# The row of RMSNorm factors from diagonal matrices instead of a power over 256 values: one core of a Trainium2 chip

## The chip, the cores and the metric

The kernel runs on one core of one Trainium2 chip. The metric is the device time in microseconds. Before the change three runs took 1470.35 us in the median.

## The reference

One decoder layer over 256 tokens (SEQ = 256) with D_MODEL = 2048, all in float32. The part that matters here is the head of the layer:

```python
def rmsnorm(x, g):
    y = x * rsqrt(mean(x * x, axis=-1) + EPS)
    return y * g

h = rmsnorm(x, norm1_g)
proj = h @ w_in
qkv, z, b_raw, a_raw, u_raw, v_raw, ga_raw, gb_raw = split(proj)
qkv = silu(causal_dwconv(qkv, dn_conv_w))
...
u = gelu(u_raw)
vg = layernorm(gelu(v_raw), sg_ln_g, sg_ln_b)
ws = where(lower triangle, sg_w, 0)
mixed = einsum(ws, vg per chunk of 128 tokens and group of 128 channels) + sg_b
y_b = u * mixed
```

Behind it follow a gated DeltaNet over q, k and v, the projections of both branches, their gated merge, an output projection, a second RMSNorm with a gated MLP, and a last RMSNorm.

The norm's factor of a token is one number, `rsqrt(mean(x*x) + EPS)`, so it is multiplied in after the projection: for products with tokens on the partitions as a column (128 partitions, one column for each of the two tiles of 128 tokens), for products with channels on the partitions as a row of 256 values that is the same on all partitions.

## The kernel before

Tokens stand in NT = 2 tiles of 128, D_MODEL in NK = 16 blocks of 128. Each float32 operand is split in a rounded part and a residual (`w_hi`, `w_lo` of the weights; the two halves of `x_h` of the activations), and a product is made of three matmuls (L153, L154, L155). The weights come through three buffers `w_raw` of 1 MB; ScalarE makes `w_hi` (L124), VectorE `w_lo` (L127), for two blocks of D_MODEL at a time. A *step* is the work on two such blocks: for u and its neighbours twelve matmuls, three for each of two blocks and two tiles of tokens. There are four buffers of `w_hi` and four of `w_lo`.

The program starts with `vg_pass`, the product for v, which also loads x, splits it, and sums its squares in `xss` (128 partitions x 2 x 256 tokens, so the sum over partitions is still missing). Then `norm1` makes the factors, in two forms. The columns `rstd1` (128x2): four small matmuls with `xss` as the stationary operand (L306), VectorE's scale and EPS (`rs_v`, L266), and a power of -0.5 on GpSimd (L267). The row `rrow` (128x256): two matmuls with a matrix of ones as the stationary operand (L303), VectorE's `rrow_v` (L312), and a power over 256 values on each partition on GpSimd (L313).

Behind it stand the four Gelu of v (L360, which need `rstd1`), VectorE's statistics of the layernorm (L361, L365), and the factor of the layernorm, `sg_rs`, again by a small power on GpSimd (L267). The ten pieces of the layernorm on VectorE (two of L372, which need `sg_rs`, and eight of L381) are written between the steps of the next product, `bau`, which has three groups: the first with 348 columns (b, a and the start of u, "u's opening group"), then two with 346. After the opening group VectorE writes `ba` (L398) and ScalarE the Gelu of u (L401); GpSimd masks the mixing matrices `ws` (L406, after their load, L405), TensorE transposes them (L412), ScalarE copies them out (L413). After the second and third group come the mixing matmuls (L421).

`rrow` is used first in the product for q, k and v, where GpSimd multiplies it in (L201 in `chan_evict`), and `pre` is the buffer of that place, whose first columns GpSimd sets to zero (L476). The second norm, far behind, makes its row in another way: `row_broadcast` (L269) multiplies the identity by a column, which gives a diagonal matrix (`dg`, L274), multiplies that by ones on TensorE (L277), so that each partition gets the whole row, and copies it out of PSUM on ScalarE (L278).

Each engine takes its instructions in order. That order is made by the tile framework's scheduler, which may place an instruction ahead of its place in the text when its own estimate says so. A wait for a value holds everything behind it on the same engine. All loads are issued by the queue of SyncE, in order.

Of the kernel before, what the change touches and what calls it, by code (L numbers as in the profile page):

```python
# [9 lines left out]
F32 = mybir.dt.float32  # L10
F32R = mybir.dt.float32r
AF = mybir.ActivationFunctionType
ALU = mybir.AluOpType
# [3 lines left out]
P = 128  # L17
D = 2048
T = 256
NT = T // P  # L20
# [9 lines left out]
EPS = 1e-6  # L30
# [68 lines left out]
def decoder_kernel(ctx: ExitStack, tc: tile.TileContext, a: dict):  # L99
    nc = tc.nc  # L100
    out = a["out"]

    const = ctx.enter_context(tc.tile_pool(name="const", bufs=1))
# [5 lines left out]
    aux = ctx.enter_context(tc.tile_pool(name="aux", bufs=4, space=PSUM))  # L109

    def bank(pool, name):
        return pool.tile([P, 512], F32, name=name, tag="bank")
# [17 lines left out]
    def source(name, g):  # L130

        cols = GROUPS[name]
        return a["w_" + name], sum(n for _, n in cols[:g]), cols[g][1]
# [23 lines left out]
    def tok_steps(x, src, n_k, name):  # L157

        ps = [bank(acc, f"{name}{t}")[:, 0 : src[2]] for t in range(NT)]
        for k0, n, hi, lo in stream(src, n_k):  # L160
            tok_mms(ps, x, n_k, k0, n, hi, lo)
            yield
        return ps

    def finish(steps):

        while True:
            try:
                next(steps)
            except StopIteration as e:  # L170
                return e.value
# [63 lines left out]
    cm = {n: cst[:, 128 * i : 128 * (i + 1)] for i, n in enumerate(CONSTS)}  # L235
    base = 128 * len(CONSTS)
    for i, n in enumerate(CONSTS64):
        cm[n] = cst[:, base + 64 * i : base + 64 * (i + 1)]
    neg_half = const.tile([P, 2 * H], F32, name="neg_half")
    nc.gpsimd.memset(neg_half, -0.5)  # L240
    eps_t = const.tile([P, 1], F32, name="eps_t")
    nc.gpsimd.memset(eps_t, EPS)
    rstd1 = const.tile([P, NT], F32, name="rstd1")
    rrow = const.tile([P, T], F32, name="rrow")

    sg_ctx = ExitStack()
# [5 lines left out]
    x_pool = x_ctx.enter_context(tc.tile_pool(name="x_t", bufs=1))  # L252
    x_t = x_pool.tile([P, NK, T], F32, name="x_t")
    xss = x_pool.tile([P, 2, T], F32, name="xss")
# [7 lines left out]
    def rsqrt_small(dst, src, scale):  # L262

        n = src.shape[-1]
        v = small.tile([P, n], F32, name="rs_v", tag=f"rs_v{n}")
        nc.vector.tensor_scalar(v, src, scalar1=scale, scalar2=EPS, op0=ALU.mult, op1=ALU.add)  # L266
        nc.gpsimd.tensor_tensor(dst, v, neg_half[:, 0:n], op=ALU.pow)  # L267

    def row_broadcast(dst, col):  # L269

        ps = bank(aux, "ps_row")
        for t in range(NT):
            dg = small.tile([P, P], F32, name="dg", tag="dg")
            nc.vector.tensor_scalar(  # L274
                dg, cm["ident"], scalar1=col[:, t : t + 1], scalar2=None, op0=ALU.mult
            )
            nc.tensor.matmul(ps[:, t * P : (t + 1) * P], lhsT=cm["ones"], rhs=dg, start=True, stop=True)  # L277
        nc.scalar.copy(dst, ps[:, 0:T])  # L278
# [19 lines left out]

    def norm1():

        ps = bank(aux, "ps_row")
        for i in range(2):
            nc.tensor.matmul(ps[:, 0:T], lhsT=cm["ones"], rhs=xss[:, i, :], start=i == 0, stop=i == 1)  # L303
        for t in range(NT):
            for i in range(2):
                nc.tensor.matmul(  # L306
                    ps[:, T + t : T + t + 1], lhsT=xss[:, i, t * P : (t + 1) * P], rhs=cm["ones"][:, 0:1],
                    start=i == 0, stop=i == 1,
                )
        rsqrt_small(rstd1, ps[:, T : T + NT], 1.0 / D)  # L310
        v = x_pool.tile([P, T], F32, name="rrow_v")
        nc.vector.tensor_scalar(v, ps[:, 0:T], scalar1=1.0 / D, scalar2=EPS, op0=ALU.mult, op1=ALU.add)  # L312
        nc.gpsimd.tensor_tensor(rrow, v, neg_half[:, 0:1].broadcast_to([P, T]), op=ALU.pow)  # L313

    def vg_pass():

# [28 lines left out]
    nc.sync.dma_start(ln_g, a["sg_ln_g"].partition_broadcast(P))  # L345
    nc.sync.dma_start(ln_b, a["sg_ln_b"].partition_broadcast(P))
    norm1()
    x_ctx.close()

# [3 lines left out]
    with sg_ctx:  # L353
        vg = sg.tile([P, NT, SGW], F32, name="vg")
        st = sg.tile([P, NT, 2, 6], F32, name="st")
        ws_t = sg.tile([P, NG, P], F32, name="ws_t")
        for c in range(2):
            for t in range(NT):
                o = vg[:, t, 512 * c : 512 * (c + 1)]
                nc.scalar.activation(o, ps_vg[c][t], AF.Gelu, scale=rstd1[:, t : t + 1])  # L360
                nc.vector.bn_stats(st[:, t, c, :], o)  # L361

        mv = sg.tile([P, NT, 2], F32, name="mv")
        for t in range(NT):
            nc.vector.bn_aggr(mv[:, t, :], st[:, t].rearrange("p c s -> p (c s)"))  # L365
        rs = sg.tile([P, NT], F32, name="sg_rs")
        rsqrt_small(rs, mv[:, :, 1], 1.0)

        def norm():

            for t in range(NT):
                nc.vector.tensor_scalar(  # L372
                    vg[:, t, :], vg[:, t, :], scalar1=mv[:, t, 0:1], scalar2=rs[:, t : t + 1],
                    op0=ALU.subtract, op1=ALU.mult,
                )
                yield
            for t in range(NT):
                for q in range(2):
                    qs = slice(512 * q, 512 * (q + 1))
                    for tab, op in ((ln_g, ALU.mult), (ln_b, ALU.add)):  # L380
                        nc.vector.tensor_tensor(vg[:, t, qs], vg[:, t, qs], tab[:, qs], op=op)  # L381
                        yield

        pieces = norm()
        ug = sg.tile([P, NT, SGW], F32, name="ug")
        for c, (start, width) in enumerate(GROUPS["bau"]):
            steps = tok_steps(x_h, source("bau", c), NK, "ps_u_")
            for _ in range(3 if c == 0 else 0):
                next(steps)
            for _ in range((5, 5, 0)[c]):  # L390
                next(pieces)
                next(steps)
            ps = finish(steps)
            n0 = max(0, C_U - start)
            u0 = start + n0 - C_U
            for t in range(NT):
                if n0:
                    nc.vector.tensor_scalar(  # L398
                        ba[:, t], ps[t][:, 0:n0], scalar1=rstd1[:, t : t + 1], scalar2=None, op0=ALU.mult
                    )  # L400
                nc.scalar.activation(  # L401
                    ug[:, t, u0 : u0 + width - n0], ps[t][:, n0:], AF.Gelu, scale=rstd1[:, t : t + 1]
                )
            if c == 0:
                nc.sync.dma_start(ws, a["sg_w"].rearrange("g i j -> i g j"))  # L405
                nc.gpsimd.affine_select(  # L406
                    ws, ws, pattern=[[0, NG], [-1, P]], compare_op=ALU.is_ge, fill=0.0, base=0, channel_multiplier=1
                )
                for q in range(2):
                    pw = bank(aux, "ps_ws")  # L410
                    for g in range(4):
                        nc.tensor.transpose(pw[:, g * P : (g + 1) * P], ws[:, 4 * q + g, :], cm["ident"])  # L412
                    nc.scalar.copy(ws_t[:, 4 * q : 4 * q + 4, :], pw.rearrange("p (g i) -> p g i", g=4))  # L413
                continue
            for t in range(NT):
                uh = ug[:, t, 512 * (c - 1) : 512 * c]
                pm = bank(aux, "ps_mix")
                for g in range(4):
                    gg = 4 * (c - 1) + g
                    gs = slice(g * P, (g + 1) * P)  # L420
                    nc.tensor.matmul(  # L421
                        pm[:, gs], lhsT=ws_t[:, gg, :], rhs=vg[:, t, gg * P : (gg + 1) * P], start=True, stop=True
                    )
                for g in range(4):
                    gg = 4 * (c - 1) + g
                    gs = slice(g * P, (g + 1) * P)
                    nc.vector.scalar_tensor_tensor(
                        uh[:, gs], pm[:, gs], sgbt[:, gg : gg + 1], uh[:, gs], op0=ALU.add, op1=ALU.mult
                    )
                to_chan(uh, y_b, t, 4 * (c - 1))  # L430
# [423 lines left out]
    for c in range(4):  # L854
        cs = slice(512 * c, 512 * (c + 1))
        ps = finish(wo_steps if c == 0 else tok_steps(x_m, source("out", c), NK, "ps_wo"))
# [18 lines left out]
    for f in range(0, NF, 2):  # L875
        ps = chan_group(x_h2, source("gu", f // 2), "ps_gu")
# [6 lines left out]
        for i in range(2):  # L883
# [8 lines left out]
            for j in range(2):  # L892
                nc.vector.scalar_tensor_tensor(
                    cv, gu[:, 0, 2 + j : 2 + j + T], fcw[:, 3 * ff + j : 3 * ff + j + 1], cv,
                    op0=ALU.mult, op1=ALU.add,
# [130 lines left out]
```

## Time and profile before

| | |
|---|---|
| three runs | 1470.35 us median, 1468.33 to 1471.92 |
| profiled execution | 1468.47 us, span of the core 1466.7 us |
| mean granted TensorE clock | 0.985 |
| busy: TensorE, VectorE, ScalarE, GpSimd | 1420.0, 899.5, 717.6, 266.1 us |
| read from HBM | 263.73 MB, 181 GB/s over the span |

The span runs from the first to the last instruction; the time of an execution has 1.8 us more around it. A row of the timeline is: start in us, duration in us, engine, line of the kernel, operation, output <- inputs, form, count, and in brackets how long the engine was idle before and who released it. A row of the waits is: who waited <- for whom, total us, times, longest us. In the groups of one line, three numbers are the shortest, median and longest duration in ns, then the first and last start in us. PE is TensorE, PEld its weight loads, DVE VectorE, ACT ScalarE, POOL GpSimd.

### The profile page before, as it was taken

What the parts mean: (1) busy time and instruction counts of PE and PEld (TensorE: products, weight loads), DVE (VectorE), ACT (ScalarE), POOL (GpSimd) and SP (SyncE); (2) the same over time, 40 slices, a digit from 0 to 9 for tenths busy, and PEclk for the clock granted to TensorE, in tenths of its full rate; (3) what the DMA queues carried; (4) which work ended last, traced back from release to release, by engine and by line L of the source; (5) the groups of instructions that cost most, each with busy time, mean ns of one, the idle gap of its engine ahead of it and who ended that gap; (6) DMA issues with size and microseconds to landing.
All of it is one profiled execution on the core that took longest, in us unless ns stands there. A gap on an engine that the chain in (4) does not pass through costs nothing.

```text
span 1466.7 us, 19565 instructions
## 1 busy us (share of the span) xinstructions
PE 1420.0 (97%) x7784; PEld 1211.3 (83%) x7784; DVE 899.5 (61%) x1128; ACT 717.6 (49%) x979; POOL 266.1 (18%) x214
## 2 busy tenths in 40 slices
PE   9739999999999999999999999999999999999997
PEld 7639888888788888888888888888888888888886
DVE  7335687868745654565557666566666666545455
ACT  7314665654344354445555555555555455444444
POOL 0560121221102200110013123122132131000002
PEclk9859999999999999999999999999999999999999
DMA  8516455444543355575555555555555555555552
GB/s 291 179 58 204 173 192 184 173 170 147 198 144 123 111 197 193 183 261 195 179 194 175 199 191 183 202 180 193 195 180 199 184 189 200 186 191 197 199 185 105
DMA packets 46620, 267.10 MB, mean 182 GB/s; under 512 B 4800, under 2 KB 12736, under 8 KB 16960
## 3 DMA queue, kind: packets, MB, share of 16 engines
q1 hardware_dynamic: 46096, 264.79, 51.4%
q8 instruction: 61, 1.00, 0.3%
q10 hardware_dynamic: 432, 1.06, 0.2%
q14 instruction: 31, 0.25, 0.0%
HBM read 263.73 MB, written 2.10 MB: 181 GB/s over the span
## 4 chain that ended last, share of the span: by engine, by line
PE 92%; issue 3%; DVE 3%; POOL 1%; DMA 0%; ACT 0%; POOLq 0%; DVEq 0%; SPq 0%
PE ps_gu L186 22%; PE ps_gu L189 11%; PE ps_qkv L186 6%; PE ps_dn L919 5%; PE ps_dn L920 5%; PE ps_dn L918 5%; PE ps_gate L153 4%; PE ps_gate L154 3%; PE ps_gate L155 3%; PE ps_qkv L189 3%; PE ps_wo L155 2%; PE ps_wo L154 2%; PE ps_wo L153 2%; PE ps_br L154 2%; PE ps_br L153 2%
## 5 line engine op out<-in xcount | busy, mean ns | idle before, releaser
L127 DVE TENSOR_TENSOR w_lo<-w_raw,w_hi 128x1024 fp32r<-128x1024 f32 (+3 forms) x412 | 529.8, 1290 | 360.8 <-ACT w_hi L124 358.5
L124 ACT CAST w_hi<-w_raw 128x1024 fp32r<-128x1024 f32 (+3 forms) x411 | 421.5, 1027 | 493.9 <-PE ps_gu L186 156.7
L186 PE MATMUL ps_gu<-x_h,w_hi 128*128 128x512 f32 x1408 | 488.5, 394 | 0.0
L189 PE MATMUL ps_gu<-x_h,w_lo 128*128 128x256 f32 x1408 | 391.3, 278 | 0.0
L186 PEld LDWEIGHTS ps_gu<-x_h,w_hi 128*128 128x128 f32 x1408 | 264.5, 188 | 61.0
L189 PEld LDWEIGHTS ps_gu<-x_h,w_lo 128*128 128x128 f32 x1408 | 264.6, 188 | 0.0
L127 DVE TENSOR_TENSOR w_lo<-wd_raw,w_hi 128x1024 fp32r<-128x1024 f32 x84 | 104.2, 1240 | 105.2 <-ACT w_hi L124 105.2
L124 ACT CAST w_hi<-wd_raw 128x1024 fp32r<-128x1024 f32 x84 | 88.6, 1054 | 120.3 <-PE ps_dn L920 113.1
L186 PE MATMUL ps_qkv<-x_h,w_hi 128*128 128x512 f32 x384 | 133.6, 395 | 0.0
L920 PE MATMUL ps_dn<-w_hi,y_s 128*128 128x512 f32 x336 | 130.9, 390 | 0.0
L918 PE MATMUL ps_dn<-w_hi,y_s 128*128 128x512 f32 x336 | 130.9, 390 | 0.0
L919 PE MATMUL ps_dn<-w_lo,y_s 128*128 128x512 f32 x336 | 130.9, 390 | 0.0
L201 POOL TENSOR_TENSOR gu<-gu,rrow 128x512 f32<-128x512 f32 x44 | 61.4, 1396 | 337.1 <-DVE gu L200 316.1
L189 PE MATMUL ps_qkv<-x_h,w_lo 128*128 128x256 f32 x384 | 106.8, 278 | 0.0
L153 PE MATMUL ps_gate<-w_hi,x_h 128*128 128x512 f32 x256 | 102.2, 399 | 0.0
L154 PE MATMUL ps_gate<-w_lo,x_h 128*128 128x512 f32 x256 | 100.2, 391 | 0.4 <-DVE w_lo L127 0.4
L155 PE MATMUL ps_gate<-w_hi,x_h 128*128 128x512 f32 x256 | 99.9, 390 | 0.0
L186 PEld LDWEIGHTS ps_qkv<-x_h,w_hi 128*128 128x128 f32 x384 | 72.2, 188 | 16.5
L918 PEld LDWEIGHTS ps_dn<-w_hi,y_s 128*128 128x128 f32 x336 | 63.1, 188 | 13.2
L919 PEld LDWEIGHTS ps_dn<-w_lo,y_s 128*128 128x128 f32 x336 | 63.1, 188 | 13.0
L920 PEld LDWEIGHTS ps_dn<-w_hi,y_s 128*128 128x128 f32 x336 | 63.1, 188 | 13.0
L189 PEld LDWEIGHTS ps_qkv<-x_h,w_lo 128*128 128x128 f32 x384 | 72.2, 188 | 0.2
(266 smaller groups left out, 1872.4 us busy)
## 6 DMA issues: line engine op xcount, KB each, us to landing
w_raw<-in_w_gu SPq DMA_DIRECT2D x88, 1024.0 KB, 4.8
wd_raw<-in_ffn_w_down SPq DMA_DIRECT2D x44, 1024.0 KB, 4.8
w_raw<-in_w_qkv SPq DMA_DIRECT2D x24, 1024.0 KB, 4.8
w_raw<-in_w_gb SPq DMA_DIRECT2D x16, 1024.0 KB, 4.8
w_raw<-in_w_ga SPq DMA_DIRECT2D x16, 1024.0 KB, 4.8
w_raw<-in_w_out SPq DMA_DIRECT2D x16, 1024.0 KB, 4.8
w_raw<-in_w_branch_b SPq DMA_DIRECT2D x8, 1024.0 KB, 4.8
w_raw<-in_w_z SPq DMA_DIRECT2D x8, 1024.0 KB, 4.8
```

What stands on the lines that cost most here:

```text
L124: nc.scalar.copy(hi, raw)
L127: nc.vector.tensor_tensor(lo, raw, f32(hi), op=ALU.subtract)
L153: nc.tensor.matmul(ps[t], lhsT=xh, rhs=hi[:, j, :], start=(k == 0), stop=False)
L154: nc.tensor.matmul(ps[t], lhsT=xh, rhs=lo[:, j, :], start=False, stop=False)
L155: nc.tensor.matmul(ps[t], lhsT=xl, rhs=hi[:, j, :], start=False, stop=(k == n_k - 1))
L186: nc.tensor.matmul(ps[m], lhsT=hi[:, j, ms], rhs=xk, start=(k == 0), stop=(k == NK - 1), skip_group_check=True)
L189: nc.tensor.matmul(ps[m][:, 0:T], lhsT=lo[:, j, ms], rhs=xk[:, 0:T], start=False, stop=(k == NK - 1), skip_group_check=True,)
L201: nc.gpsimd.tensor_tensor(dst, dst, bc(rrow, 1, 2), op=ALU.mult)
L918: nc.tensor.matmul(o, lhsT=yh, rhs=hi[:, cs], start=(k == 0), stop=False)
L919: nc.tensor.matmul(o, lhsT=yh, rhs=lo[:, cs], start=False, stop=False)
L920: nc.tensor.matmul(o, lhsT=yl, rhs=hi[:, cs], start=False, stop=(k == NF - 1))
```

## The change

The factors' row is no longer computed for itself. `norm1` keeps only the columns, with a new one-column constant `one_c` in place of a column of the loaded ones. After u's opening group `row_broadcast`, which the second norm has used already, makes the row from the two columns of `rstd1`. Two operations on `rstd1` before anything needs it (a product, and a power on two values) run at the program's start; their result is overwritten.

```diff
+    one_c = const.tile([P, 1], F32, name="one_c")
+    nc.gpsimd.memset(one_c, 1.0)
     neg_half = const.tile([P, 2 * H], F32, name="neg_half")
...
     rstd1 = const.tile([P, NT], F32, name="rstd1")
+    nc.gpsimd.tensor_tensor(rstd1, neg_half[:, 0:1].broadcast_to([P, NT]), neg_half[:, 0:NT], op=ALU.mult)
+    nc.gpsimd.tensor_tensor(rstd1, rstd1, neg_half[:, 0:NT], op=ALU.pow)
...
     def norm1():
 
-        ps = bank(aux, "ps_row")
-        for i in range(2):
-            nc.tensor.matmul(ps[:, 0:T], lhsT=cm["ones"], rhs=xss[:, i, :], start=i == 0, stop=i == 1)
+        ps = bank(aux, "ps_ss")
         for t in range(NT):
             for i in range(2):
                 nc.tensor.matmul(
-                    ps[:, T + t : T + t + 1], lhsT=xss[:, i, t * P : (t + 1) * P], rhs=cm["ones"][:, 0:1],
+                    ps[:, t : t + 1], lhsT=xss[:, i, t * P : (t + 1) * P], rhs=one_c,
                     start=i == 0, stop=i == 1,
                 )
-        rsqrt_small(rstd1, ps[:, T : T + NT], 1.0 / D)
-        v = x_pool.tile([P, T], F32, name="rrow_v")
-        nc.vector.tensor_scalar(v, ps[:, 0:T], scalar1=1.0 / D, scalar2=EPS, op0=ALU.mult, op1=ALU.add)
-        nc.gpsimd.tensor_tensor(rrow, v, neg_half[:, 0:1].broadcast_to([P, T]), op=ALU.pow)
+        rsqrt_small(rstd1, ps[:, 0:NT], 1.0 / D)
...
             if c == 0:
+                row_broadcast(rrow, rstd1)
                 nc.sync.dma_start(ws, a["sg_w"].rearrange("g i j -> i g j"))
```

The lines shift with the change: `rsqrt_small`'s power stands at L271 then, the diagonals at L278, their products at L281, the copy at L282, the layernorm's pieces at L371 and L380.

The scheduler moves some instructions along. On GpSimd, before and in the change, from the first constant of this place to the layernorm's factor (`one_c`, `neg_half`, `rstd`, `sg_rs` are the constants and factors named above, the number behind a name is that of the buffer):

```order
L240 MEMSET neg_half 128x16
L242 MEMSET eps_t 128x1
L267 ISA
L267 TENSOR_TENSOR rstd_109<-rs_v,neg_half 128x2
L313 TENSOR_TENSOR rrow<-rrow_v,neg_half 128x256
L406 AFFINE_SELECT ws<-ws 128x1024
L476 MEMSET pre 128x2x4 x2
L267 TENSOR_TENSOR sg_rs<-rs_v,neg_half 128x2
```

The changed program has, at the same place:

```order
L242 MEMSET neg_half 128x16
L244 MEMSET eps_t 128x1
L246 ISA
L246 TENSOR_TENSOR rstd_111<-neg_half 128x2
L247 TENSOR_TENSOR rstd_111<-rstd_111,neg_half 128x2
L476 MEMSET pre 128x2x4 x2
L271 TENSOR_TENSOR rstd_111<-rs_v,neg_half 128x2
L406 AFFINE_SELECT ws<-ws 128x1024
L271 TENSOR_TENSOR sg_rs<-rs_v,neg_half 128x2
```

The wide power left, two operations came to the front, and the memsets of `pre` moved ahead of `rstd`, because `pre` lies in memory that x and `xss` give free, and no longer over `rrow_v`.

On VectorE, from the residuals of u's opening group to the statistics of the layernorm (`rs_v` is the scaled sum, `st` and `mv` the statistics), before:

```order
L127 TENSOR_TENSOR w_lo<-w_raw,w_hi 128x2x348 x4
L266 TENSOR_SCALAR rs_v<-ps_row 128x2
L312 TENSOR_SCALAR rrow_v<-ps_row 128x256
L361 BN_STATS st<-vg 128x6 x4
L365 BN_AGGR mv<-st 128x2
```

and changed:

```order
L127 TENSOR_TENSOR w_lo<-w_raw,w_hi 128x2x348 x3
L270 TENSOR_SCALAR rs_v<-ps_ss 128x2
L278 TENSOR_SCALAR dg<-cst,rstd_111 128x128 x2
L127 TENSOR_TENSOR w_lo<-w_raw,w_hi 128x2x348
L360 BN_STATS st<-vg 128x6 x4
L364 BN_AGGR mv<-st 128x2
```

The diagonals are made as soon as `rstd1` is there, not where they are written, and one `w_lo` moved behind them.

On TensorE, at the end of the product for v and at the end of u's opening group (`ps_ws` are the transposes of the mask, the last rows the start of the second group), before:

```order
L303 MATMUL ps_row<-xss,cst 128x256 x2
L306 MATMUL ps_row<-cst,xss 128x1 x4
L153 MATMUL ps_u_531<-w_hi,x_h 128x348
...
L155 MATMUL ps_u_532<-w_hi,x_h 128x348
L412 MATMUL ps_ws<-cst,ws 128x128 x8
L153 MATMUL ps_u_693<-w_hi,x_h 128x346
```

and changed:

```order
L308 MATMUL ps_ss<-one_c,xss 128x1 x4
L153 MATMUL ps_u_530<-w_hi,x_h 128x348
...
L155 MATMUL ps_u_531<-w_hi,x_h 128x348
L281 MATMUL ps_row<-dg,cst 128x128 x2
L412 MATMUL ps_ws<-cst,ws 128x128 x8
L153 MATMUL ps_u_700<-w_hi,x_h 128x346
```

The two wide matmuls of the sum left the first place, and the two with the diagonals came to the second.

## The prediction

> **What bounds the kernel now.** I read the page first: busy time and the slices.
>
> ```profile
> span 1466.7 us, 19565 instructions
> PE 1420.0 (97%) x7784; PEld 1211.3 (83%) x7784; DVE 899.5 (61%) x1128; ACT 717.6 (49%) x979; POOL 266.1 (18%) x214
> PE   9739999999999999999999999999999999999997
> POOL 0560121221102200110013123122132131000002
> ```
>
> TensorE is busy nearly throughout, so the time falls only where TensorE stands still or runs slowly. It does so in the second and third slice (36.67 us each), the very slices where GpSimd has its largest digits but one thing to do. So I asked the chain of releasers, the waits between 40 and 140 us, who held TensorE.
>
> ```profile
> PE ps_u L154 <- DVE w_lo L127: 35.3, 1, 35.3
> DVE vg L372 <- POOL sg_rs L267: 37.9, 1, 37.9
> ```
>
> One wait of 35.3 us by TensorE for a weight residual `w_lo` of VectorE, and one of 37.9 us by VectorE for GpSimd's `sg_rs`. The next three views, in order of time by engine, show why: GpSimd, then VectorE, then TensorE.
>
> ```profile
> 51.75 0.70 POOL L267 TENSOR_TENSOR rstd<-rs_v,neg_half 128x2 f32<-128x2 f32 x1 [50.69 <-DVE rs_v L266]
> 52.42 41.14 POOL L313 TENSOR_TENSOR rrow<-rrow_v,neg_half 128x256 f32<-128x256 f32 x1
> 93.52 1.10 POOL L406 TENSOR_SCALAR_AFFINE_SELECT ws<-ws 128x1024 f32<-128x1024 f32 x1
> 94.56 0.14 POOL L476 MEMSET pre<- 128x8 f32 x2
> 94.67 0.70 POOL L267 TENSOR_TENSOR sg_rs<-rs_v,neg_half 128x2 f32<-128x2 f32 x1
> ...
> 51.52 0.41 DVE L312 TENSOR_SCALAR rrow_v<-ps_row 128x256 f32<-128x256 f32 x1
> 53.20 2.47 DVE L361 BATCH_NORM_STATS2 st<-vg 128x6 f32<-128x512 f32 x4 [1.28 <-ACT vg L360]
> 55.70 0.83 DVE L127 TENSOR_TENSOR w_lo<-w_raw,w_hi 128x696 fp32r<-128x696 f32 x1
> 57.31 0.16 DVE L266 TENSOR_SCALAR rs_v<-mv 128x2 f32<-128x2 f32 x1
> 95.40 1.54 DVE L372 TENSOR_SCALAR vg<-vg,mv,sg_rs 128x1024 f32<-128x1024 f32 x2 [37.92 <-POOL sg_rs L267]
> 97.45 0.88 DVE L127 TENSOR_TENSOR w_lo<-w_raw,w_hi 128x696 fp32r<-128x696 f32 x1
> ...
> 49.59 1.02 PE L303 MATMUL ps_row<-xss,cst 128*128 128x256 f32 x4
> 50.45 0.95 PE L306 MATMUL ps_row<-cst,xss 128*128 128x1 f32 x8
> 51.26 0.41 PE L153 MATMUL ps_u<-w_hi,x_h 128*128 128x348 f32 x1
> 62.75 0.32 PE L153 MATMUL ps_u<-w_hi,x_h 128*128 128x348 f32 x1
> 98.38 0.66 PE L154 MATMUL ps_u<-w_lo,x_h 128*128 128x348 f32 x1 [35.32 <-DVE w_lo L127]
> 103.35 0.32 PE L153 MATMUL ps_u<-w_hi,x_h 128*128 128x348 f32 x1
> 105.09 0.41 PE L153 MATMUL ps_u<-w_hi,x_h 128*128 128x346 f32 x1
> ```
>
> The reader is to see a convoy. GpSimd runs the power over 256 values for 41.14 us. The second small power, `sg_rs`, whose input is ready at 57.31 + 0.16 = 57.47 us, stands behind it until 94.67. VectorE takes its work in order, stands before L372, and the seventh `w_lo` of u's first group stands behind that. TensorE has done six steps (72 matmuls from 51.26 to 62.75, 0.1596 us each) and one matmul of the seventh, and then waits for that `w_lo`.
>
> Afterwards TensorE is slow as well as late: 17 matmuls take from 98.38 to 103.35, 4.97 us, where 17 x 0.1596 = 2.71 are due. The windows show the clock and that nothing else of this size remains:
>
> ```profile
> 64.00:98.00 34.00, 0.00 (x0) 0.00 (x0) 2.60 (x4) 0.00 (x0) 31.36 (x5) 0.52 0.00 0
> 98.00:104.00 6.00, 5.62 (x22) 5.62 (x23) 6.00 (x10) 0.77 (x1) 0.00 (x0) 0.57 0.37 112
> 104.00:140.00 36.00, 36.00 (x238) 35.58 (x237) 20.86 (x33) 18.93 (x27) 0.00 (x0) 1.00 0.63 201
> ```
>
> The columns are length, busy time of PE, PEld, DVE, ACT, POOL, then granted clock, DMA share and GB/s. The clock is 0.57 of full between 98 and 104 and 1.00 behind it, where TensorE is busy for all of 36 us.
>
> **The change, part by part.**
>
> *The power goes.* Its duration is a matter of its values, by the other powers:
>
> ```profile
> L267 POOL TENSOR_TENSOR r<-rs_v,neg_half x2: 547/550/553, 1451.5 to 1459.6; 128x1 f32<-128x1 f32 x2
> L267 POOL TENSOR_TENSOR nrm<-rs_v,neg_half x2: 2913/2914/2915, 300.9 to 339.4; 128x16 f32<-128x16 f32 x2
> ```
>
> From 1 to 16 values it grows by (2.914 - 0.550)/15 = 0.158 us a value, so 256 values make 0.550 + 255 x 0.158 = 40.7 us, and 41.14 was measured. The record is work, not a hidden wait, and goes with the instruction.
>
> In GpSimd's order, shown above, two dummy operations on two values come in near the start, where GpSimd was idle for 50.69 us by its row at 51.75 (0.70 us each at most, hidden); the two memsets of `pre` have moved ahead of `rstd`. They need the norm's last matmul, which `rs_v` needs too, so they run beside `rs_v` (0.14 us against 0.16) and I cost them at nothing; without that cover, 0.14 us, off the path. `sg_rs` now stands only behind the mask of `ws`, and that behind the load of `ws`:
>
> ```profile
> L405 SPq DMA_DIRECT2D ws<-in_sg_w x1: 613/613/613, 47.9 to 47.9; - x1
> DMA to landing us min/median/max: 5.5/5.5/5.5
> ```
>
> It lands at 47.9 + 5.5 = 53.4 us; with 1.10 for the mask GpSimd is free at 54.5, 3 us before `sg_rs` has its input at 57.47. So `sg_rs` starts at once.
>
> *Does TensorE then stop at all?* What one diagonal and one piece of the norm cost stands in these rows, the diagonal's from the second norm:
>
> ```profile
> L274 DVE TENSOR_SCALAR dg<-cst,rstd x2: 278/283/288, 732.3 to 732.9; 128x128 f32<-128x128 f32 x2
> 98.25 0.68 DVE L381 TENSOR_TENSOR vg<-vg,ln_b 128x512 f32<-128x512 f32 x1
> ```
>
> The two diagonals stand early, not behind the group, and they add a wait: VectorE stops for GpSimd's `rstd`, with the fourth `w_lo` and the statistics behind it. `rstd` was ready at 51.75 + 0.70 = 52.45; the norm's matmuls end 0.86 us earlier now (below), so 51.6. Two diagonals and one `w_lo` end by 51.6 + 2 x 0.28 + 0.88 = 53.0, before the statistics began (53.20), and the fourth `w_lo` is due on TensorE only with step four, at about 50.4 + 36 x 0.1596 = 56.1. So this wait costs nothing, and the chain to `sg_rs` is no later than before: 57.47, plus 0.70 and about 0.1 on each side, 58.4. From the start of L372 to the end of the seventh `w_lo` it took 97.45 + 0.88 - 95.40 = 2.93, hence 61.3. TensorE asks for it at 62.91 - 0.86 = 62.05. The margin is about 0.75 us: thin, but positive, and the later ones gain, since each step of TensorE lasts 12 x 0.1596 = 1.92 while VectorE needs 0.88 and one or two pieces of the norm of 0.68.
>
> *So the stop goes:* from the matmul at 62.75 its successor is due at 62.91 and came at 98.38: 35.47 us. *The slow clock goes with it:* 4.97 - 2.71 = 2.26 us. The Trainium skill, in "TensorE: Matmul & The Clock Gate", Part 1, says that the array runs at half rate after an idle window of about 3.4 us, and at full rate again after as much sustained work; by that rule the penalty is an estimated 1.7 us and the sum would be 0.6 smaller. The trace agrees in kind, with 4.97 us of slow work.
>
> *TensorE's own work.* By TensorE's order above, the wide sum is gone from the end of the v pass, and two products with the diagonals stand behind u's opening group. The wide sum held TensorE from 49.59 to 50.45: 0.86 us saved. The products are the same as those of the second norm, quoted here with the copy of their row, and with two casts of ScalarE behind the place where the new copy goes:
>
> ```profile
> 751.84 0.61 PE L277 MATMUL ps_row<-dg,cst 128*128 128x128 f32 x4
> 752.21 0.47 PE L186 MATMUL ps_gu<-x_h,w_hi 128*128 128x512 f32 x1
> 752.88 0.36 ACT L278 COPY rrow<-ps_row 128x256 f32<-128x256 f32 x1
> 107.33 0.77 ACT L124 CAST w_hi<-w_raw 128x692 fp32r<-128x692 f32 x1 [0.23 <-ACT ws_t L413]
> 109.25 0.77 ACT L124 CAST w_hi<-w_raw 128x692 fp32r<-128x692 f32 x1 [1.15 <-PE ps_u L155]
> ```
>
> TensorE goes on 752.21 - 751.84 = 0.37 us later: a cost on the path, since the diagonals are ready long before. ScalarE's copy, 0.36 us, delays the cast that stood at 107.33; the next cast then idles 1.15 us for TensorE, which shows ScalarE ahead there, so I cost the copy at nothing. Uncovered it would be 0.36. `rrow` is first used far behind this place.
>
> *Loads.* Without the pause the queue no longer gets 35 us for free. Weights of u come at
>
> ```profile
> w_raw<-in_w_bau SPq DMA_DIRECT2D x8, 692.0 KB, 4.6
> ```
>
> 4.6 us to land, for 2 x 1.92 = 3.84 us of matmuls, with three buffers. The window from 104 to 140 holds the same loads without a pause, and TensorE was never idle in it. So loads cost nothing; the bound is the second rival.
>
> **The sum:** 35.47 + 2.26 + 0.86 - 0.37 = 38.2 us. The profiled execution took 1468.47 us around its span of 1466.7, so 1430.2; it is 1.9 below the median of the runs (1470.35, from 1468.33 to 1471.92), from which the sum gives 1432.1. I take 1431.2, between them.
>
> **Rivals.**
> 1. *A remnant of the stop.* The margin of 0.75 us is used up by a later landing of `ws`, a slower `rs_v`, or VectorE held by GpSimd's mask for its 1.10 us. Then TensorE waits 0.4 to 4 us at the same `w_lo`: 1431.6 to 1435. For it: the thin margin. Against it: the estimate takes no credit for the earlier matmuls on VectorE's side. The Trainium skill, "SBUF — State Buffer", "Who interferes with whom", has VectorE operations with two SBUF inputs and GpSimd exclude each other for a whole instruction. The row at 55.70 speaks against such a hold here: `w_lo` took 0.83 us in the middle of the power, and 0.88 at 97.45 outside it.
> 2. *Loads become the bound of u.* If loads went one by one, each would miss 4.6 - 3.84 = 0.8 us, over the 8 of this size 6 us: 1437. Against it: the window from 104 to 140.
> 3. *The change does not do what it says:* the 41 us belong to something that stays, and the next GpSimd instruction inherits them: 1470. Against it: the fit by values above.
> 4. *Slower:* `sg_rs`, and with it VectorE's queue and the seventh `w_lo`, now hangs on the load of `ws`, through the mask ahead of it. The mask began at 93.52 before; with the 0.14 of the memsets, now ahead, and the 0.49 that TensorE's own work saves, the time is as before if `ws` lands at 94.2 us and longer by each microsecond past that, 1476 for a landing at 100. At 53.4 the point is 40 us away.
>
> **Chances.** Forecast 0.84, remnant 0.11, loads 0.03, no effect 0.01, slower 0.01. The first three are all faster by over 0.2% (2.9 us, what a measurement of this kernel can tell): faster 0.98, same 0.01, slower 0.01. The range starts from the runs' own spread around the sum (1468.33 - 38.2 = 1430.1 to 1471.92 - 38.2 = 1433.7); below, I allow 2.5 us for what no row prices (the added constant moves all later buffers in memory, the banks of PSUM rotate otherwise), above, 3 us for the remnant: 1427.6 to 1436.7.
>
> **What would show it.** Right: no idle of TensorE over 1 us between 50 and 70, clock 1.00 there, GpSimd's `sg_rs` near 57, the group from 346 columns starting at about 105.09 - 38.2 = 66.9 us, `rrow` written by ScalarE near 68. Wrong: TensorE waiting for `w_lo` L127 in u's first group (remnant), ScalarE's casts waiting for loads of u (loads), or a long row of GpSimd in place of L313.

## The result, and the profile after

The changed kernel takes 1431.66 us (median; 1431.63 to 1431.94), the kernel before 1469.62 beside it (1468.33 to 1471.92): a ratio of 0.974, with an interval from 0.9724 to 0.9757. The profiled execution took 1431.63 us around a span of 1429.9. The forecast was 1431.2, with 1427.6 to 1436.7 as its range. In some executions, at an unchanged clock, the stage of q, k and v, or in two kernels that of gate and up, runs about 2% slower, which moves a time by 2 to 3 or by 9 us and is taken up at the end.

The page of after, busy times and slices, with the clock's row:

```profile
span 1429.9 us, 19571 instructions
PE 1418.3 (99%) x7784; PEld 1209.0 (85%) x7784; DVE 899.5 (63%) x1129; ACT 717.9 (50%) x980; POOL 226.3 (16%) x216
PE   9999999999999999999999999999999999999997
POOL 0001211221021200200032231322322221000002
PEclk9999999999999999999999999999999999999999
```

TensorE's busy time is what it was, to 1.7 us (1420.0 before); its share rose because the span shrank. The hole in its second and third digit is gone, and with it the 5 and the 6 in GpSimd's row. The windows of after in the stretch where TensorE had stood (columns as before: length, PE, PEld, DVE, ACT, POOL, granted clock, DMA share, GB/s):

```profile
40.00:60.00 20.00, 20.00 (x111) 18.24 (x110) 10.89 (x20) 10.18 (x14) 2.87 (x5) 1.00 0.74 246
60.00:80.00 20.00, 20.00 (x131) 20.00 (x131) 14.31 (x22) 9.64 (x15) 0.00 (x0) 1.00 0.60 183
80.00:100.00 20.00, 20.00 (x134) 19.80 (x133) 12.07 (x19) 9.72 (x14) 0.00 (x0) 1.00 0.61 211
```

TensorE is busy for all of the 60 us, at a clock of 1.00. The timelines of GpSimd, VectorE, TensorE and ScalarE, in that order, show the convoy dissolved:

```profile
51.50 0.70 POOL L271 TENSOR_TENSOR rstd<-rs_v,neg_half 128x2 f32<-128x2 f32 x1
53.15 1.32 POOL L406 TENSOR_SCALAR_AFFINE_SELECT ws<-ws 128x1024 f32<-128x1024 f32 x1 [0.94 <-DMA ws<-in_sg_w]
57.78 0.69 POOL L271 TENSOR_TENSOR sg_rs<-rs_v,neg_half 128x2 f32<-128x2 f32 x1 [3.31 <-DVE rs_v L270]
...
52.24 0.48 DVE L278 TENSOR_SCALAR dg<-cst,rstd 128x128 f32<-128x128 f32 x2 [0.89 <-POOL rstd L271]
52.64 0.88 DVE L127 TENSOR_TENSOR w_lo<-w_raw,w_hi 128x696 fp32r<-128x696 f32 x1
57.54 0.16 DVE L270 TENSOR_SCALAR rs_v<-mv 128x2 f32<-128x2 f32 x1
58.52 1.54 DVE L371 TENSOR_SCALAR vg<-vg,mv,sg_rs 128x1024 f32<-128x1024 f32 x2 [0.81 <-POOL sg_rs L271]
60.57 0.88 DVE L127 TENSOR_TENSOR w_lo<-w_raw,w_hi 128x696 fp32r<-128x696 f32 x1
...
49.98 0.40 PE L155 MATMUL ps_vg<-w_hi,x_h 128*128 128x512 f32 x1
62.66 0.32 PE L154 MATMUL ps_u<-w_lo,x_h 128*128 128x348 f32 x1
66.31 0.60 PE L281 MATMUL ps_row<-dg,cst 128*128 128x128 f32 x4
66.75 1.04 PE L412 MATMUL ps_ws<-cst,ws 128*128 128x128 f32 x8
67.54 0.41 PE L153 MATMUL ps_u<-w_hi,x_h 128*128 128x346 f32 x1
1420.17 0.39 PE L920 MATMUL ps_dn<-wz,y_s 128*128 128x512 f32 x1
...
69.32 0.37 ACT L282 COPY rrow<-ps_row 128x256 f32<-128x256 f32 x1
```

GpSimd now idles 3.31 us before `sg_rs` and waits for its input, instead of the input waiting 37 us for GpSimd. VectorE waits 0.81 us for `sg_rs`, not 37.92. The seventh `w_lo` ends at 60.57 + 0.88 = 61.45, and TensorE uses it at 62.66.

### The profile page after: what moved, and what is told of

It reads as the page before. It is cut to its first block, busy times and chain, and to the rows that moved or that the text cites. A ratio compares the mean times of both kernels' runs of the same rounds, so it can differ in the third digit from the quotient of the medians.

```text
span 1429.9 us, 19571 instructions
## 1 busy us (share of the span) xinstructions
PE 1418.3 (99%) x7784; PEld 1209.0 (85%) x7784; DVE 899.5 (63%) x1129; ACT 717.9 (50%) x980; POOL 226.3 (16%) x216
## 4 chain that ended last, share of the span: by engine, by line
PE 94%; DVE 3%; DMA 1%; POOL 1%; issue 1%; ACT 0%; SPq 0%; POOLq 0%; DVEq 0%; ACTq 0%
PE ps_gu L186 23%; PE ps_gu L189 11%; PE ps_qkv L186 6%; PE ps_dn L918 5%; PE ps_dn L919 5%; PE ps_dn L920 5%; PE ps_gate L153 4%; PE ps_gate L154 4%; PE ps_gate L155 3%; PE ps_qkv L189 3%; PE ps_wo L153 2%; PE ps_wo L154 2%; PE ps_wo L155 2%; PE ps_br L154 2%; PE ps_br L153 2%; PE ps_br L155 2%
## 5 line engine op out<-in xcount | busy, mean ns | idle before, releaser
L186 PE MATMUL ps_gu<-x_h,w_hi 128*128 128x512 f32 x1408 | 488.5, 394 | 0.0
L186 PEld LDWEIGHTS ps_gu<-x_h,w_hi 128*128 128x128 f32 x1408 | 264.0, 187 | 61.1
L186 PE MATMUL ps_qkv<-x_h,w_hi 128*128 128x512 f32 x384 | 133.6, 394 | 0.0
L186 PEld LDWEIGHTS ps_qkv<-x_h,w_hi 128*128 128x128 f32 x384 | 72.0, 188 | 16.4
```

Source lines behind the costliest of these rows:

```text
L186: nc.tensor.matmul(ps[m], lhsT=hi[:, j, ms], rhs=xk, start=(k == 0), stop=(k == NK - 1), skip_group_check=True)
```

## The experiments

The theory: the 41 us power costs nothing by itself; it cost by its place, ahead of `sg_rs` in GpSimd's row, through VectorE's order, for whatever exceeds the margin of the seventh `w_lo`, plus a slow clock. Rivals: that its work (GpSimd beside VectorE, SBUF held), or the lateness of `rrow`, was the cost, or that another part of the change brought the gain.

**Order alone.** The kernel before, with the dummy operations and the same power over 256 values, only behind `sg_rs` (its exponent is made from `sg_rs`, so that it can't start sooner); no diagonals.

```
     rsqrt_small(rs, mv[:, :, 1], 1.0)
+    nc.gpsimd.tensor_scalar(nh2, rs[:, 0:1], scalar1=0.0, scalar2=-0.5, op0=ALU.mult, op1=ALU.add)
+    nc.gpsimd.tensor_tensor(rrow, rrow_v, nh2.broadcast_to([P, T]), op=ALU.pow)
```

> The power over 256 values, the wide sum and rrow_v stay as before the change; only the power's place on GpSimd moves behind sg_rs (its exponent is made from sg_rs), and the two dummy operations stand at the start as in the change. Theory 'place': the power's 41 us cost nothing by themselves, only sg_rs standing behind them did; the stop (35.5 us) and the slow clock (2.3) go, the wide sum (0.86) stays and the diagonals' products (0.37) are not there, so 1431.7 + 0.5 = 1432.2 us, at most 1434. Rival 'work': GpSimd's 41 us hold VectorE or the clock back wherever they stand, most of all the layernorm's pieces with two inputs in SBUF that now run beside them: 1450 to 1470 us, and the pieces and w_lo take longer than 0.68 and 0.88 us.

Measured: 1441.39 us, ratio 0.9794 (0.9777 to 0.981). That is neither the theory's number nor the rival's. Its window over the stretch where TensorE had stood, and two rows of its GpSimd and one of its VectorE:

```profile
49.00:106.00 57.00, 57.00 (x373) 56.01 (x372) 39.31 (x65) 29.39 (x41) 44.31 (x7) 1.00 0.62 198
...
58.16 0.69 POOL L271 TENSOR_TENSOR sg_rs<-rs_v,neg_half 128x2 f32<-128x2 f32 x1 [1.76 <-DVE rs_v L270]
59.22 41.47 POOL L371 TENSOR_TENSOR rrow<-rrow_v,nh 128x256 f32<-128x256 f32 x1
...
61.25 0.87 DVE L127 TENSOR_TENSOR w_lo<-w_raw,w_hi 128x696 fp32r<-128x696 f32 x1
```

Where the power runs, TensorE is busy 57.00 of 57 us at full clock: the stop is gone with the power still there, 41.47 us long. The 10 us missing were lost elsewhere, without a gap: this group of the page shows more time for the same 1408 matmuls of gate and up, and the second line, from after, is its counterpart.

```profile
L186 PE MATMUL ps_gu<-x_h,w_hi 128*128 128x512 f32 x1408 | 497.4, 398 | 0.0
```

```profile
L186 PE MATMUL ps_gu<-x_h,w_hi 128*128 128x512 f32 x1408 | 488.5, 394 | 0.0
```

So 8.9 us lie in gate and up; q, k and v took 137.3 us from the first to the last matmul of its line L186, against 134.7. Whether the power had anything to do with that was settled by the next run.

**Order alone, in place.** The same, but the power works in `rrow` itself and the exponent's tile is one that is released early, so that all weights lie where they lie in the kernel before.

```
-    v = x_pool.tile([P, T], F32, name="rrow_v")
-    nc.vector.tensor_scalar(v, ps[:, 0:T], ...)
-    nc.gpsimd.tensor_tensor(rrow, v, neg_half[:, 0:1].broadcast_to([P, T]), op=ALU.pow)
+    nc.vector.tensor_scalar(rrow, ps[:, 0:T], ...)
...
+    nc.gpsimd.tensor_tensor(rrow, rrow, nh2.broadcast_to([P, T]), op=ALU.pow)
```

> The power over 256 values is kept and only its place is changed, as in the run with order alone, but it works in rrow itself, so that every tile keeps the address that it has in the kernel before. If the place is what costs, and the 9 us that the stage of gate and up lost in the earlier form came of that form's addresses: the changed kernel's 1431.7 less its diagonals' products of 0.44, 1431.2 us, or 1433.5 where the q, k and v stage runs at its slower 137.3 us (2.3 more). If a 41 us power on GpSimd, or the order of the PSUM banks, is what slowed gate and up: about 1440 to 1443 again, with pairs of 0.353 us there.

Measured: 1431.12 us, ratio 0.9741 (0.9727 to 0.9756), no different from the change's 0.974. GpSimd, then the end of the v pass and the start of the second group on TensorE:

```profile
57.76 0.70 POOL L269 TENSOR_TENSOR sg_rs<-rs_v,neg_half 128x2 f32<-128x2 f32 x1 [4.04 <-DVE rs_v L268]
58.81 41.48 POOL L370 TENSOR_TENSOR rrow<-rrow,nh 128x256 f32<-128x256 f32 x1
...
49.56 0.39 PE L155 MATMUL ps_vg<-w_hi,x_h 128*128 128x512 f32 x1
67.54 0.41 PE L153 MATMUL ps_u<-w_hi,x_h 128*128 128x346 f32 x1
```

The whole gain comes from moving 41 us of GpSimd's work behind an operation of 0.70 us. The rival that the work itself holds VectorE back had forecast longer residuals and longer pieces of the layernorm beside the power; in this run the residuals took 0.87 us and the pieces with two inputs 0.68, as in the changed kernel, and only one piece took longer, by 0.29 us (the last section shows it). What the diagonals add is TensorE's: from the last matmul of v to the second group it is 67.54 - 49.56 = 17.98 us here and 67.54 - 49.98 = 17.56 in after, 0.42 less, as 0.86 for the wide sum less 0.44 for the products would have it. In whole times that isn't resolved: 1431.12 against 1431.66 and, in a later repetition, 1431.24.

**A dose of the old wait.** The changed kernel, with a power over n values that nobody reads put back ahead of `sg_rs`, n = 48, 128 and 256.

```
         rsqrt_small(rstd1, ps[:, 0:NT], 1.0 / D)
+        nc.gpsimd.tensor_tensor(
+            dose, rstd1[:, 0:1].broadcast_to([P, n]), neg_half[:, 0:1].broadcast_to([P, n]), op=ALU.pow
+        )
```

> The changed kernel with a power over 48 values that nobody reads, in GpSimd's row ahead of the mask on ws and so ahead of sg_rs: 0.55 + 47 x 0.158 = 8.0 us by the rows of the powers. Theory of the place: sg_rs comes 3.5 us later than now (GpSimd was idle for the rest), the 7th w_lo with it, and that has 1.2 us to spare (62.66 less 61.45): TensorE stops for 2.3 us, too short for a slower clock, 1434.0 us. Rival, the power costs for its work on GpSimd and not for what stands behind it: no stop and 1431.7.

> The changed kernel with an unread power over 128 values ahead of sg_rs: 0.55 + 127 x 0.158 = 20.6 us, by the run with 256 (41.13, sg_rs 36.6 later than in the changed kernel) 20.6 too. Theory of the place: sg_rs 16.1 us later, a stop of 16.1 less 1.2 = 14.9 us; with a slow stretch of the clock worth 1.5 (as behind the stop of 2.2 us) to 2.3 (as in the kernel before): 1448.1 to 1448.9. Rival, work and not place, or a threshold: a time that doesn't stand between those with 48 and 256 in proportion to sg_rs's delay.

> The same with a power over all 256 values, 0.55 + 255 x 0.158 = 40.8 us, ahead of sg_rs, while the row still comes from the diagonals. Theory of the place: sg_rs 36.4 us later, a stop of 36.4 less 1.2 = 35.2 us and a slow stretch of the clock worth 2.3 behind it: 1469.2 us, the old time without the old use of the power. Rival, it was the row's lateness at its readers (rrow) and not sg_rs: 1431.7, since here the row is as early as in the changed kernel.

The dose, `sg_rs` and TensorE's wait in the profiles of the three, in this order:

```profile
52.31 8.00 POOL L314 TENSOR_TENSOR dose<-rstd,neg_half 128x48 f32<-128x48 f32 x1
61.34 0.70 POOL L272 TENSOR_TENSOR sg_rs<-rs_v,neg_half 128x2 f32<-128x2 f32 x1
PE ps_u L154 <- DVE w_lo L127: 2.2, 1, 2.2
```

```profile
52.62 20.73 POOL L314 TENSOR_TENSOR dose<-rstd,neg_half 128x128 f32<-128x128 f32 x1
74.37 0.70 POOL L272 TENSOR_TENSOR sg_rs<-rs_v,neg_half 128x2 f32<-128x2 f32 x1
PE ps_u L154 <- DVE w_lo L127: 15.3, 1, 15.3
```

```profile
52.19 41.13 POOL L314 TENSOR_TENSOR dose<-rstd,neg_half 128x256 f32<-128x256 f32 x1
94.34 0.70 POOL L272 TENSOR_TENSOR sg_rs<-rs_v,neg_half 128x2 f32<-128x2 f32 x1
PE ps_u L154 <- DVE w_lo L127: 35.3, 1, 35.3
```

| values | `sg_rs` later than in after (57.78) | TensorE's stop | difference | time | ratio |
|---|---|---|---|---|---|
| 48 | 3.56 us | 2.2 | 1.4 | 1433.99 | 0.9759 (0.9744 to 0.9774) |
| 128 | 16.59 | 15.3 | 1.3 | 1448.60 | 0.9858 (0.9843 to 0.9872) |
| 256 | 36.56 | 35.3 | 1.3 | 1468.55 | 1.0 (0.999 to 1.0009) |

The stop is `sg_rs`'s delay less a constant 1.3 to 1.4 us, the margin that the seventh `w_lo` has. With 256 values the time of the kernel before comes back in full, though the row still comes from the diagonals: `rrow`'s lateness was never the cost.

**The dummies.** In the kernel before, alone; and the changed kernel without them.

```
     rstd1 = const.tile([P, NT], F32, name="rstd1")
+    nc.gpsimd.tensor_tensor(rstd1, neg_half[:, 0:1].broadcast_to([P, NT]), neg_half[:, 0:NT], op=ALU.mult)
+    nc.gpsimd.tensor_tensor(rstd1, rstd1, neg_half[:, 0:NT], op=ALU.pow)
```

> The kernel before with nothing but the two dummy operations on rstd1 at the start. Theory 'place': same as before, 1468 to 1472 us. Rival 'first use': the dummies take a first-use cost of the power off the path, and are worth some us by themselves: below 1466 us.

> The change without the two dummy operations. The scheduler then lets ScalarE make seven w_hi ahead of the Gelu instead of four, and puts the power's setup behind the memsets of pre. Theory 'place': no change in time, 1431.7 within 1 us, since seven w_lo stand ahead of the wait for sg_rs now; the first power takes 0.70 us as ever. Rival 'first use': the first power or its setup takes some us longer at about 51 us, the Gelu and sg_rs come late by it, and TensorE waits again in u's groups: 1434 to 1440 us.

Measured: 1471.14 us, ratio 1.0 (0.999 to 1.001), for the dummies alone. Without them three executions took 1433.66 to 1434.08 us, ratio 0.9745 (0.9729 to 0.9761); a fourth took 3671.3 us, which nothing on record explains, and the ratio leaves it out. The three lie about 2 us above the change, outside the forecast of 1431.7 within 1. In the profile the excess sits in q, k and v, again 137.3 us in place of 134.7. It can't be put down to the missing dummies: the profile with the dummies alone shows that stage at 137.2 as well. In the stretch that the dummies could touch, from the last matmul of v to the second group, it is 67.20 - 49.63 = 17.57 us without them and 17.56 with them. The dummies are worth nothing that shows.

**The diagonals' products early**, at the end of the v pass rather than behind the group.

```
         rsqrt_small(rstd1, ps[:, 0:NT], 1.0 / D)
+        row_broadcast(rrow, rstd1)
...
-                row_broadcast(rrow, rstd1)
```

> The change with the row made from the diagonals at once in norm1, not behind u's opening group; TensorE has the two products five matmuls into that group, before the diagonals are there (52.7 us in the change, TensorE at 51.8). Theory 'place': TensorE waits about 0.9 to 1.5 us there, too short for a slow clock: 1432.6 to 1433.2 us. Rival 'the place behind the group does not matter': 1431.7 within 0.3 us.

Measured: 1433.11 us (1431.85 to 1434.57), ratio 0.9741 (0.9726 to 0.9755). In its profile (1432.02 us):

```profile
52.22 0.68 PE L281 MATMUL ps_row<-dg,cst 128*128 128x128 f32 x4 [0.57 <-PE ps_u L154]
...
51.83 0.48 DVE L278 TENSOR_SCALAR dg<-cst,rstd 128x128 f32<-128x128 f32 x2 [0.89 <-POOL rstd L271]
```

TensorE stands 0.57 us there. The releaser named is its own earlier matmul, long done; by the times it lacked the diagonals, which VectorE made from 51.83 to 52.31. From the last matmul of v to the second group this run took 67.96 - 49.57 = 18.39 us, 0.83 more than the change. So "behind the opening group" is worth 0.8 us; the whole time can't tell that from nothing.

**Where the first run with order alone lost its 9 us.** Three runs: the changed kernel with a tile of 256 values that shifts the weights to that run's addresses; the in-place form with a tile of 264 values, for its addresses and its PSUM banks; and that run's own program again.

```
     rrow = const.tile([P, T], F32, name="rrow")
+    pad = const.tile([P, 256], F32, name="pad")
+    nc.gpsimd.memset(pad, 0.0)
```

> The changed kernel with one more tile of 256 values a partition that nothing reads, which moves the split weights and x_h by 1024 bytes, to the very addresses that they have in the run with order alone (its power stays gone). If those addresses cost that run its 9 us in gate and up: 1431.7 + 9.0 = 1440.7 us, and gate and up 498 instead of 489 us. If they don't: 1431.7, or 1434.0 with a slower q, k and v stage.

> The order-only form that works in rrow itself, with a tile of 264 values a partition ahead of the weights, so that the split weights and x_h stand at the addresses of the first order-only form and the PSUM tiles in its banks. If the two together slow gate and up: 1440 us, 498 us in that stage. If not: 1431.1, or 1433.5.

> The run with order alone in its first form, once more, on another occasion. If its 9 us in gate and up belong to that program (an interplay of its tiles' places that neither e5 nor e6 has): 1440.2 to 1442.7 us and 498 us for gate and up again. If they belong to the chip or the hour of that run: 1431.1, or 1433.5 with a slower q, k and v stage, and 489 us.

Measured: 1431.26 us, ratio 0.974 (0.9725 to 0.9754), for the first, so in these four executions the addresses alone did nothing. The second took 1432.0 once and 1439.9 to 1440.6 three times (ratio 0.9781, 0.975 to 0.9813). The old program, unchanged, took 1431.17, 1433.90, 1440.31 and 1440.54 (0.9775, 0.9743 to 0.9806), and its profile, of the 1431.17, has gate and up at normal speed:

```profile
L186 PE MATMUL ps_gu<-x_h,w_hi 128*128 128x512 f32 x1408 | 488.9, 391 | 0.0
```

So the 9 us are no fixed cost of that program, nor of the power alone, which the in-place run has too. They came in 9 of the 12 runs of the two programs that have both its addresses and its banks, and in none of 4 with the addresses alone and of 4 with the banks alone. Those 8 ran on another chip than the 12, and the 4 with the addresses alone lack the power as well. That the pair of them invites the loss is suggested, not shown, and why is open.

**The changed kernel again**, beside those.

> The changed kernel again, beside the others on the same chip: 1431.7 us, 1434.0 where the q, k and v stage runs slower. Against the order-only form (1431.12) it should stand 0.4 above, for its four products; less than that means that the work removed is worth nothing beyond what the diagonals cost.

Measured: 1431.24 us (1431.12 to 1431.54), ratio 0.9739 (0.9725 to 0.9754). It stands 0.1 above the order-only form, not 0.4; the two ran on different chips, and that form's own runs spread over 2.5 us (1430.62 to 1433.15), so neither can be told.

## Why the prediction was right

- **The stop.** The step that carried 35.47 us held: no wait of TensorE for a `w_lo` is left between 40 and 140 us, and the dose over 256 values puts exactly 35.3 back. The reason held as well: place, not work.
- **The margin**, estimated at 0.75 us, was 62.66 - 61.45 = 1.2, and 1.3 to 1.4 by the doses. Against the clock, `w_lo` came 0.15 later than forecast and TensorE's asking 0.6 later, since the v pass ended at 49.98, not 49.36. Counted from the end of the v pass, TensorE asked as forecast, and it was `w_lo` that came 0.47 earlier: the input of `sg_rs` was ready 57.54 + 0.16 - 49.98 = 7.72 us behind it, where the kernel before had 57.47 - 49.36 = 8.11. So the part estimated too long was the chain to `sg_rs`: the prediction has it "no later than before" and takes no credit for the earlier matmuls of the norm. In the repeated profile of the changed kernel the v pass ends at 49.48, and the margin is again 1.2. So the remnant was less near than its chance of 0.11 said, though 8 us of GpSimd's time, the dose with 48 values, did bring it.
- **The slow clock** left with the stop: 1.00 in all three windows. The term of 2.26 us was one execution's: worked out in the same way (17 matmuls there, 15 and 13 in the doses), 2.1 us were lost behind the stop of 15.3 us, and 1.8 behind that of 35.3.
- **TensorE's own work.** The wide sum's 0.86 was right. The products cost 66.75 - 66.31 = 0.44, against 0.37; the row that gave 0.37 is followed by a matmul of 512 columns, these products by transposes.
- **Where the sum was too large.** From the last matmul of v to the second group the kernel before took 105.09 - 49.36 = 55.73 us, and the changed one 17.56: 38.17 less, as the sum has it. But 38.2 was forecast for the whole profiled execution, and its span fell by 36.8. The second group began at 67.54, not 66.9, for the v pass had ended 0.62 later: that lies ahead of everything the change touches, and in the repeated profile, with the v pass ending at 49.48, all but 0.1 of it is absent. From there to the last matmul it was 1420.17 - 67.54 = 1352.63, and these rows of the kernel before, the last matmul of v and the last of all,

```profile
49.36 0.39 PE L155 MATMUL ps_vg<-w_hi,x_h 128*128 128x512 f32 x1
1457.37 0.39 PE L920 MATMUL ps_dn<-wz,y_s 128*128 128x512 f32 x1
```

  give 1457.37 - 105.09 = 1352.28: 0.35 more. The tail behind it took 1429.9 - 1420.17 = 9.73 against 1466.7 - 1457.37 = 9.33, 0.4 more. These three are 1.4, all of the difference, and none is a step of the change. The forecast came within 0.5 us because it stood a microsecond above the sum, between the profiled execution and the median; that closeness is luck, the 38 us are not.
- **Costs put at nothing.** The wait for `rstd` before the diagonals came to 0.89 us on VectorE and delayed nobody on TensorE; the copy of `rrow` fell at 69.32, not near 68, behind two activations and a cast, and nothing waited for it; the loads of u kept up. `ws` landed at 53.1 (the mask began at 53.15), so the slower rival's point at 94 stayed as far off as forecast.
- **GpSimd and VectorE holding each other**, weighed with the remnant: it is seen. The mask took 1.32 us in after, 1.10 before, with a `w_lo` running until 52.64 + 0.88 = 53.52; it had 3 us of room and cost nothing.

## What to carry to other kernels

Read a long operation on an idle engine by what stands behind it in that engine's order: here 41 us of GpSimd's work cost 38 us ahead of an operation of 0.7 us, and nothing behind it. Before replacing such an operation by a cleverer one, try moving it; the rewrite was worth 0.4 us of TensorE's time beyond the move. Work out the margin of the instruction that the bound engine would wait for, since a delay costs only what exceeds it (1.3 us here, then one for one, with 1.5 to 2.3 us of slow clock behind the stop).

## What the runs showed of the hardware

- **A stop of 2.2 us was followed by a slow clock.** In the one profile with 48 values TensorE resumed at full clock and slowed about 1 us later. Two windows of it:

```profile
64.00:66.00 2.00, 0.95 (x6) 0.95 (x7) 2.00 (x4) 0.00 (x0) 0.00 (x0) 1.00 0.00 0
66.00:68.00 2.00, 2.00 (x9) 2.00 (x8) 2.00 (x4) 0.29 (x1) 0.00 (x0) 0.55 0.00 0
```

  It cost about 1.5 us, which the expectation for that run had excluded. The other runs of that kernel had spans 0.9 to 1.5 us shorter, so perhaps not all of them had it. The Trainium skill, "TensorE: Matmul & The Clock Gate", Part 1, names an idle window of about 3.4 us for this; here the slow stretch followed a shorter stop.
- **GpSimd and VectorE lengthened some of each other's operations, and not others.** In the run with the products early, `sg_rs` met a residual of VectorE, an operation with two inputs:

```profile
56.78 1.41 POOL L271 TENSOR_TENSOR sg_rs<-rs_v,neg_half 128x2 f32<-128x2 f32 x1 [1.46 <-DVE rs_v L270]
...
56.76 0.88 DVE L127 TENSOR_TENSOR w_lo<-w_raw,w_hi 128x696 fp32r<-128x696 f32 x1
```

  It took 1.41 us in place of 0.70, about as much longer as the residual still ran. Inside the power of 41.47 us, which had begun first, a `w_lo` took 0.87 us as ever. The Trainium skill, "SBUF — State Buffer", "Who interferes with whom", lets whichever starts first block the other; these runs agree for the residual ahead of `sg_rs`, and not for the `w_lo` inside the power.

  VectorE can be the one that takes longer, too. In the in-place run, where the power began at 58.81, the two pieces of the layernorm with one input took

```profile
58.49 1.83 DVE L375 TENSOR_SCALAR vg<-vg,mv,sg_rs 128x1024 f32<-128x1024 f32 x2 [0.82 <-POOL sg_rs L269]
```

  1.83 us together, against 1.54 in after: the first, begun ahead of the power, 0.81, the second, begun within it at 59.22, 1.10. In the profile with the dose of 256 values, which began at 52.19, a diagonal begun at 52.14 took 0.74 us; none took over 0.29 in after. Why these were held and the residuals were not is open.
- **Matmuls can run 2% slower for a whole stage, with TensorE busy throughout and the clock at 1.00** (gate and up 497.4 against 488.5 us by the groups above), in one execution of a program and not in the next. Differences of 2 to 9 us between kernels that share such a stage need their stage lengths compared before a cause is named.
